# Gate matrices from two-byte one-hots in three parts, with eight more early strips, in a two-layer model kernel

## The chip, the cores and the metric

One core of one Trainium2 chip runs the whole program as one launch. The metric is device time in microseconds, median of several runs on the chip; the kernel before takes 3077.76 us (median of 3, 3073.26 to 3085.12).

## What is computed

The reference is a two-layer model on 512 tokens of width 1024, in float32. Layer one: a mixer (a wide depthwise convolution, a short gated convolution and a spatial gate between two matrix products), a product-key expert layer (PEER), and an embedding gate; then a state-space mixer, a gated feed-forward, another embedding gate, differential attention, a second feed-forward and gate, and a final norm. The change lies almost wholly in the expert layer:

```
q = (nf @ w_q).reshape(t, 8, 256)
s1, s2 = q[..., :128] . sub_keys[:, 0],  q[..., 128:] . sub_keys[:, 1]   # 128 scores each
v1, i1 = top_k(s1, 16);  v2, i2 = top_k(s2, 16)
vals, ci = top_k((v1[..., :, None] + v2[..., None, :]).reshape(t, 8, 256), 16)
idx = i1[ci // 16] * 128 + i2[ci % 16]          # 128 experts of 16384 for each token
gates = softmax(vals)
act = gelu(x . expert_u[idx]) * gates
out = sum_k act * expert_v[idx]
```

## The kernel before, in words

Activations lie features on partitions, tokens along the free dimension. Matrix products are made to nearly float32 accuracy from three fp32r products (`mm3`, L159: high and low part of the weights, high and low part of the input). A *strip* is 1024 rows by 128 columns of weights, 512 KB, loaded on SP's queue (`dma_to`, L128), split into parts on ScalarE (L148) and on VectorE or GpSimd (L150), and used in 24 products.

Program order is written by hand. After each strip `tick` (L97) runs what `later(n, f)` (L92) has put n ticks ahead, and `run_bg` (L200) then issues background items from a list, each with a cost, until the credit given for a strip is used. Every engine runs its instructions in this order.

The expert layer treats block 0 of 128 tokens by gathering rows (`first_block`, L965) and the other 384 tokens densely, over all 16384 experts in 128 strips of `expert_u` and 128 of `expert_v`:

- Stage one (`peer`, L624): the queries, the scores, the top 16 of each half, and the first 9 dense `expert_u` strips. The bias table of the attention is prepared here too (`bias_prep`, L1741), in the background.
- The gates stage: `plan_choice` (L781) picks the experts. `top` takes the best 16 of 50 candidate pairs of a head; `look` (L835) turns a candidate number into an expert number by a one-hot comparison (L838, VectorE), a product with the codes (L841, GpSimd) and a sum over the candidates (L845, VectorE). `soft`, `soft2` make the gates, `ints` (L854) splits an expert number into e1 and e2 of 128 each, and `trans` (L865) turns e1, e2 and the gates on TensorE so that the 128 choices of a token lie on partitions, with the token along the free dimension. `plan_gates` (L878) then makes, for eight tokens at a time, 48 times, the dense gate matrix G[e2, e1] of each token: `front` writes the one-hot of e2 (L894), a one-hot of e1 (L902) and its product with the gate (four tokens on ScalarE, L906, four on VectorE, L908), `mid` makes one fp32 product a token (L917), and `back` copies it on ScalarE (L924) into `gb`, from which pieces go to DRAM (L932). Numbers 0 to 127 for the comparisons are held in a bank of PSUM of their own (`iotaP`, L641).
- Meanwhile TensorE has R - 9 = 47 further `expert_u` strips, whose gelu (L705) is stored to DRAM (`sd`). R = 56 (L575) strips are thus made early; `ahead` (L601) spreads them over the 128. The background credit of a strip is the sum of the costs divided by the strips (L732). 32 row steps of block 0 (`early`, L982: a gather and a dot product) are mixed into blocks 2 and 3 of the background.
- The dense stage (`dense`, L1033): for each e, the `expert_u` strip where it was not made early (gelu L1086, then the gate product L1076), or a load of its stored gelu; then 18 products with the strip of `expert_v` into six banks (L1112). The rest of block 0 and the preparation of the state-space layer run in the background.

Elsewhere: `lin2` (L183) makes the first two strips of a stage from inputs that are only just being written, the first all but its last part, then the second; with `first`, used once, it interleaves the two. `head_ln` and `two_rms` (L332, L355) are the normalisation by head of the mixer, a chain of TensorE, ScalarE and VectorE steps one tick apart; L444 starts it when a convolution is done.

Of the kernel before, what the change touches and what calls it, by code (L numbers as in the profile page):

```python
# [36 lines left out]
class K:  # L37
# [294 lines left out]
    def head_ln(self, y, out):  # L332
# [22 lines left out]
    def two_rms(self, sq, sel, scale, out):  # L355
# [28 lines left out]
        self.later(1, turn)  # L384
# [14 lines left out]
    def mix_in(self, after):  # L399
# [32 lines left out]
        def conv(j, sg):  # L432
# [4 lines left out]
            def tap(k):  # L437
# [5 lines left out]
                if k == 0:  # L443
                    self.later(1, lambda: self.head_ln(acc, lambda yn: ln_a(j, yn)))  # L444
# [82 lines left out]
        self.lin2(xn, posts[o[0]], posts[o[1]], first=True)  # L527
# [47 lines left out]
    R = 56  # L575
    EARLY = 32
    SLOW = 1.6
    RB = 1
    GG = 4
    TC = 32  # L580
    HT = 8
    NV = 4
# [41 lines left out]
    def peer(self):  # L624
# [16 lines left out]
        iotaP = self.bank("mmc", (P, P), "held")  # L641
# [7 lines left out]
        self.bg = self.bias_prep() + [(0.1, lambda: nc.scalar.copy(iotaP, iota))]  # L649
# [131 lines left out]
    def plan_choice(self, vals, idx, iota, rc):  # L781
# [5 lines left out]
        self.eT = e1T, e2T, gT = [loc((P, TD), tag=t) for t in ("e1T", "e2T", "gT")]  # L787
        state = {}

        def part(b, half):  # L790
# [42 lines left out]
            sh = [P, 16, NCD]  # L833

            def look(h):  # L835
                if h < 4 * half + 4:
                    eq = loc((P, 16, NCD), tag="eq", bufs=1 + self.LG)
                    nc.vector.tensor_tensor(  # L838
                        eq, d["i"][:, h, :].unsqueeze(2).to_broadcast(sh), iota[:, 0:NCD].unsqueeze(1).to_broadcast(sh), ALU.is_equal
                    )  # L840
                    nc.gpsimd.tensor_tensor(eq, eq, d["k"][:, h, :].unsqueeze(1).to_broadcast(sh), ALU.mult)  # L841
                    d["eq", h] = eq
# [7 lines left out]
            if not half:  # L850
                return items
            items.insert(len(items) - 3, (0.5, soft2))

# [11 lines left out]
            def trans():  # L865
                pt = self.px_((P, 3, P), "pt")
# [4 lines left out]
                for j, t in enumerate((e1T, e2T, gT)):  # L871
# [6 lines left out]
    def plan_gates(self, part, iota, iotaP, gd, step):  # L878
# [3 lines left out]
        A = HT - self.NV  # L882
        e1T, e2T, gT = self.eT
# [5 lines left out]

        def front(i):  # L890
            t0 = i * HT
            sh = [P, HT, P]
            oh2 = self.loc((P, HT, P), tag="oh2", bufs=2)
            nc.vector.tensor_tensor(  # L894
                oh2, e2T[:, t0 : t0 + HT].unsqueeze(2).to_broadcast(sh), iotaP.unsqueeze(1).to_broadcast(sh), ALU.is_equal
            )
            gh = self.loc((P, HT, P), tag="gh", bufs=2)
            A = HT - self.NV
            if A:
                oh1 = self.loc((P, P, A), BF16, tag="oh1", bufs=2)  # L900
                sh1 = [P, P, A]
                nc.vector.tensor_tensor(oh1, e1T[:, t0 : t0 + A].unsqueeze(1).to_broadcast(sh1), iotaP.unsqueeze(2).to_broadcast(sh1), ALU.is_equal)  # L902
            for t in range(HT):
                e1, g = e1T[:, t0 + t : t0 + t + 1], gT[:, t0 + t : t0 + t + 1]
                if t < A:
                    nc.scalar.activation(gh[:, t, :], oh1[:, :, t], AF.Copy, scale=g)  # L906
                else:
                    nc.vector.tensor_scalar(out=gh[:, t, :], in0=iota, scalar1=e1, scalar2=g, op0=ALU.is_equal, op1=ALU.mult)  # L908
# [29 lines left out]
        bg = part(1, 1)  # L938
        nxt = {1: choose(0) + choose(2), 2: choose(3), 3: []} if self.EARLY else {1: choose(2), 2: choose(3), 3: choose(0)}
        rows = [(1.2, lambda i=i: step(i)) for i in range(self.EARLY)]  # L940
        for b in range(1, NB):
# [7 lines left out]
            for j in range(k):  # L949
# [6 lines left out]
                m = -(-len(more) // (k - j))  # L956
                bg += more[:m]
                more = more[m:]
        bg += [(0.0, lambda: mid(n - 1)), (0.0, lambda: back(n - 2)), (0.0, lambda: back(n - 1)), (0.0, rest)]
# [73 lines left out]
    def dense(self, nr, gd, sd, xd, step):  # L1033
# [707 lines left out]
    def bias_prep(self):  # L1741
# [8 lines left out]
        def loads():  # L1750
            nc.gpsimd.memset(rb, 1e30)
# [429 lines left out]
```

## Time and profile before

| | |
|---|---|
| Median of 3 runs | 3077.76 us (3073.26 to 3085.12) |
| Profiled execution, its own time | 3078.27 us |
| Span of its trace, first to last instruction | 3076.5 us |
| Granted TensorE clock, mean | 0.971 of full |
| TensorE busy | 2908.9 us, 95% |
| VectorE, ScalarE, GpSimd busy | 2218.9, 1303.4, 1093.8 us |
| DRAM read, written | 468.75, 63.44 MB |

Busy time is the union of an engine's instructions, so it hides differences between stages; matrix products are pipelined, and their rate is read from start to start. A wait is put down to what came last before the instruction started. An idle engine costs nothing unless the engine that bounds the stage waits for it.

### The profile page before, as it was taken

The numbers are of one execution on the slowest core, as the hardware profiler recorded it, in microseconds if no ns is written. First come the engines' busy times: TensorE is split into PE (matmuls) and PEld (weight loads), VectorE is DVE, ScalarE is ACT, GpSimd is POOL, SyncE is SP. The second block draws the span as 40 slices with busy tenths as digits, with TensorE's granted clock in tenths as the row PEclk, the third lists the DMA queues.
The fourth block names the chain that finished last, engine by engine and source line by source line (L and its number), as shares of the span: only waits on it lengthen the run. The fifth ranks groups of instructions, "written<-read, shape, count | busy, mean of one in ns | idle before, by whom it ended". The sixth has DMA issues, their size and how long they took to land. (4 is left out here: it accounts for less than half of the span.)

```text
span 3076.5 us, 39413 instructions
## 1 busy us (share of the span) xinstructions
PE 2908.9 (95%) x14359; PEld 2445.6 (79%) x14359; DVE 2218.9 (72%) x3788; ACT 1303.4 (42%) x2209; POOL 1093.8 (36%) x936
## 2 busy tenths in 40 slices
PE   8999988889999999999999979999999998999998
PEld 6677888788887888888787768888877766888886
DVE  7945888986888889988886674666666356566665
ACT  4333246566433433443335343433344345433333
POOL 3224566653248778877872321000011011100001
PEclk9889999899999999999999989999999989999999
DMA  4124335679778988898894473233332211333323
GB/s 140 48 83 148 97 129 186 232 245 313 252 263 313 336 318 322 331 350 315 312 328 147 125 225 103 77 102 99 99 97 95 77 42 42 96 103 96 96 72 99
DMA packets 235067, 534.77 MB, mean 174 GB/s; under 512 B 35135, under 2 KB 127683, under 8 KB 222202
## 3 DMA queue, kind: packets, MB, share of 16 engines
q1 hardware_dynamic: 170570, 343.69, 33.9%
q0 software_dynamic: 24832, 140.74, 12.4%
q10 hardware_dynamic: 39472, 47.84, 4.5%
q8 instruction: 113, 1.85, 0.2%
q14 instruction: 80, 0.66, 0.1%
HBM read 468.75 MB, written 63.44 MB: 173 GB/s over the span
## 5 line engine op out<-in xcount | busy, mean ns | idle before, releaser
L150 DVE TENSOR_TENSOR wl<-wr,wh 128x1024 fp32r<-128x1024 f32 (+2 forms) x453 | 545.3, 1213 | 510.1 <-ACT wh L148 509.9
L148 ACT ACTIVATE wh<-wr 128x1024 fp32r<-128x1024 f32 (+2 forms) x552 | 544.7, 995 | 403.7 <-PE mm L163 196.2
L161 PE MATMUL mm<-xn,wh 128*128 128x512 f32 x1296 | 520.9, 402 | 14.3 <-ACT xn L119 8.9
L163 PE MATMUL mm<-xn,wh 128*128 128x512 f32 x1296 | 512.4, 395 | 5.8 <-DVE xn L114 5.8
L162 PE MATMUL mm<-xn,wl 128*128 128x512 f32 x1296 | 512.1, 395 | 1.9 <-POOL wl L150 1.9
L230 POOL TENSOR_TENSOR accs<-accs,sq 128x512 f32<-128x512 f32 x56 | 86.3, 1541 | 1042.7 <-ACT sq L229 1038.4
L1112 PE MATMUL pv<-wh,A 128*128 128x512 f32 x1536 | 437.5, 397 | 15.8 <-ACT A L117 5.9
L150 POOL TENSOR_TENSOR wl<-wr,wh 128x1024 fp32r<-128x1024 f32 x99 | 241.3, 2439 | 449.1 <-ACT wh L148 446.6
L161 PE MATMUL mm<-n,wh 128*128 128x384 f32 x1024 | 350.6, 342 | 0.8 <-ACT gs L705 0.8
L162 PE MATMUL mm<-n,wl 128*128 128x384 f32 x1024 | 345.6, 337 | 5.9 <-DVE wl L150 4.3
L1112 PEld LDWEIGHTS pv<-wh,A 128*128 128x128 f32 x1536 | 286.8, 189 | 80.6 <-DVE A L112 11.0
L163 PE MATMUL mm<-n,wh 128*128 128x384 f32 x1024 | 345.9, 338 | 3.1 <-DVE n L114 3.1
L161 PEld LDWEIGHTS mm<-xn,wh 128*128 128x128 f32 x1296 | 248.5, 192 | 69.3 <-ACT xn L119 8.9
L163 PEld LDWEIGHTS mm<-xn,wh 128*128 128x128 f32 x1296 | 247.7, 191 | 61.4 <-DVE xn L114 8.3
L162 PEld LDWEIGHTS mm<-xn,wl 128*128 128x128 f32 x1296 | 248.4, 192 | 55.2 <-POOL wl L150 2.3
L1112 PE MATMUL pv<-wl,A 128*128 128x512 f32 x768 | 241.9, 396 | 9.4 <-DVE wl L150 9.3
L117 ACT ACTIVATE A<-ga 128x384 fp32r<-128x384 f32 x128 | 67.3, 526 | 357.7 <-DVE ga L1076 357.7
L162 PEld LDWEIGHTS mm<-n,wl 128*128 128x128 f32 x1024 | 194.2, 190 | 9.7 <-DVE wl L150 5.6
L161 PEld LDWEIGHTS mm<-n,wh 128*128 128x128 f32 x1024 | 194.5, 190 | 4.9 <-issue 1.4
L163 PEld LDWEIGHTS mm<-n,wh 128*128 128x128 f32 x1024 | 194.0, 189 | 3.4 <-DVE n L114 3.4
L1112 PEld LDWEIGHTS pv<-wl,A 128*128 128x128 f32 x768 | 144.0, 189 | 49.0 <-DVE wl L150 17.3
L1670 ACT ACTIVATE uc<-up,vec 128x512 f32<-128x512 f32 x88 | 71.8, 816 | 203.8 <-DVE up L1668 203.8
(414 smaller groups left out, 5438.9 us busy)
## 6 DMA issues: line engine op xcount, KB each, us to landing
wr<-in_exp_u SPq DMA_DIRECT2D x128, 512.0 KB, 5.4
wr<-in_exp_v SPq DMA_DIRECT2D x128, 512.0 KB, 6.9
wr<-in_w_up SPq DMA_DIRECT2D x88, 512.0 KB, 3.6
gd<-gb ACTq DMA_DIRECT2D x48, 512.0 KB, 5.0
G<-gd SPq DMA_DIRECT2D x32, 768.0 KB, 6.3
wr<-in_w_dn SPq DMA_DIRECT2D x64, 320.0 KB, 2.9
wr<-in_w_pg SPq DMA_DIRECT2D x24, 512.0 KB, 4.2
sd<-gs SPq DMA_DIRECT2D x56, 192.0 KB, 2.9
```

What stands on the lines that cost most here:

```text
L117: nc.scalar.activation(hi, src, AF.Copy)
L148: nc.scalar.activation(s.hi, s.raw, AF.Copy)
L150: eng.tensor_tensor(s.lo, s.raw, s.hi.bitcast(F32), ALU.subtract)
L161: t.matmul(ps, wh, xh, start=start, stop=False)
L162: t.matmul(ps, wl, xh, start=False, stop=False)
L163: t.matmul(ps, wh, xl, start=False, stop=stop)
L230: self.later(1, lambda: nc.gpsimd.tensor_tensor(acc, acc, sq, ALU.add))
L1112: nc.tensor.matmul(pv[2 * b + h], a[:, x, o], w[:, h * T : h * T + T], start=(e == 0 and i == 0 and w is s.hi), stop=last)
L1670: nc.scalar.activation(c, u, AF.Identity, scale=w(2), bias=cb[:, m : m + 1])
```

## The change

- Gates: the one-hots of e2 and e1 are written as bfloat16 for all eight tokens in one instruction each, in the order (pair of tokens, number, token of the pair), so that two neighbouring elements lie side by side. The gate is split into three bfloat16 parts that sum to it (`part1` to `part3`), and the one-hot of e1 is multiplied by each: three VectorE instructions. The numbers and the turned gates (`gP`) are bfloat16 in the held bank of PSUM. `mid` makes three products a token, accumulated, and writes a token into every fourth word of the bank, so that `back` copies runs of four words in order.
- `look` compares in bfloat16 with the candidates outermost, GpSimd writes float32, and the sum reads with a step of 16 words.
- R is 64; the last 8 of the 32 row steps come after the last gates (`TAIL`). `trans` of a block stands at the end of the block before, with three items between it and `ints` in the first case; the other items end one step earlier.
- The gelu of a dense strip stays in PSUM (`p_s`), and the gate product reads it there.
- `lin2` always interleaves. In the mixer, `head_ln` starts two ticks after its convolution, and its turn comes two ticks after the statistics.
- The loads of the bias table are issued at once at the start of the expert layer, and its sign is changed on VectorE.

```
-    def lin2(self, rhs, *posts, first=False):
+    def lin2(self, rhs, *posts):
...
-        if first:
-            for k in range(n + 1):
-                for i, j in ((0, k), (1, k - 2)):
-                    if 0 <= j < n - 1:
-                        self.prod(pss[i], ss[i], rhs, j, j + 1)
-        else:
-            for s, ps in zip(ss, pss):
-                self.prod(ps, s, rhs, 0, n - 1)
+        for k in range(n + 1):
+            for i, j in ((0, k), (1, k - 2)):
+                if 0 <= j < n - 1:
+                    self.prod(pss[i], ss[i], rhs, j, j + 1)
...
-            self.later(1, lambda: self.two_rms(d["sq"], self.sel2, 1.0, scale))
+            self.later(1, lambda: self.two_rms(d["sq"], self.sel2, 1.0, scale, 2))
...
-    def two_rms(self, sq, sel, scale, out):
+    def two_rms(self, sq, sel, scale, out, lag=1):
...
-        self.later(1, turn)
+        self.later(lag, turn)
...
-                    self.later(1, lambda: self.head_ln(acc, lambda yn: ln_a(j, yn)))
+                    self.later(2, lambda: self.head_ln(acc, lambda yn: ln_a(j, yn)))
...
-    R = 56
+    R = 64
+    TAIL = 8
...
-        iotaP = self.bank("mmc", (P, P), "held")
+        held = self.bank("mmc", (P, T), "held").bitcast(BF16)
+        iotaP = held[:, 0 : 2 * P].rearrange("p (e b) -> p e b", b=2)
+        self.gP = held[:, 2 * P : 8 * P].rearrange("p (c k t) -> p c k t", c=2, k=3)
+        self.identB = self.loc((P, P), BF16, tag="identB")
+        nc.scalar.copy(self.identB, self.ident)
...
-        self.bg = self.bias_prep() + [(0.1, lambda: nc.scalar.copy(iotaP, iota))]
+        bias, loads = self.bias_prep()
+        loads()
...
+        self.bg = [(0.1, hold)] + bias
...
                 if h < 4 * half + 4:
-                    eq = loc((P, 16, NCD), tag="eq", bufs=1 + self.LG)
+                    eq = loc((P, NCD, 16), BF16, tag="eq", bufs=2)
                     nc.vector.tensor_tensor(
-                        eq, d["i"][:, h, :].unsqueeze(2).to_broadcast(sh), iota[:, 0:NCD].unsqueeze(1).to_broadcast(sh), ALU.is_equal
+                        eq.rearrange("p c (a b) -> p c a b", b=2),
+                        d["i"][:, h, :].rearrange("p (a b) -> p a b", b=2).unsqueeze(1).to_broadcast(sh),
+                        iota[:, 0:NCD, :].unsqueeze(2).to_broadcast(sh),
+                        ALU.is_equal,
                     )
-                    nc.gpsimd.tensor_tensor(eq, eq, d["k"][:, h, :].unsqueeze(1).to_broadcast(sh), ALU.mult)
+                    ec = loc((P, NCD, 16), tag="ec", bufs=1 + self.LG)
+                    nc.gpsimd.tensor_tensor(ec, eq, d["k"][:, h, :].unsqueeze(2).to_broadcast([P, NCD, 16]), ALU.mult)
...
-                    nc.vector.tensor_reduce(d["e"][:, h, :], d["eq", h], AX.X, ALU.add)
+                    nc.vector.tensor_reduce(d["e"][:, h, :], d["eq", h].rearrange("p c k -> p k c"), AX.X, ALU.add)
...
+                nc.scalar.copy(d["gp"][:, 0, :], d["gf"])
...
+                nc.gpsimd.tensor_tensor(d["gr"], d["gf"], d["gp"][:, 0, :], ALU.subtract)
+                nc.scalar.copy(d["gp"][:, 1, :], d["gr"])
...
+                nc.gpsimd.tensor_tensor(d["gp"][:, 2, :], d["gr"], d["gp"][:, 1, :], ALU.subtract)
...
-                nc.tensor.transpose(pt[:, 2, :], d["g"].rearrange("p a b -> p (a b)"), self.ident)
+                for j in range(3):
+                    nc.tensor.transpose(self.gP[:, b % 2, j, :], d["gp"][:, j, :], self.identB)
...
+        H2 = HT // 2
+        pairs = lambda t: t.rearrange("p (a b) -> p a b", b=2).unsqueeze(2).to_broadcast([P, H2, P, 2])
...
+            num = iotaP.unsqueeze(1).to_broadcast([P, H2, P, 2])
+            oh2 = self.loc((P, H2, P, 2), BF16, tag="oh2", bufs=2)
+            nc.vector.tensor_tensor(oh2, pairs(e2T[:, t0 : t0 + HT]), num, ALU.is_equal)
+            oh1 = self.loc((P, H2, P, 2), BF16, tag="oh1")
+            nc.vector.tensor_tensor(oh1, pairs(e1T[:, t0 : t0 + HT]), num, ALU.is_equal)
+            gh = self.loc((P, 3, H2, P, 2), BF16, tag="gh", bufs=2)
+            for k in range(3):
+                nc.vector.tensor_tensor(gh[:, k], oh1, pairs(self.gP[:, b % 2, k, o : o + HT]), ALU.mult)
...
-                pg = self.px_((P, 4, P), "pg")
+                pg = self.px_((P, P, 4), "pg")
                 for t in range(4 * q, 4 * q + 4):
-                    nc.tensor.matmul(pg[:, t % 4, :], oh2[:, t, :], gh[:, t, :], start=True, stop=True)
+                    for k in range(3):
+                        nc.tensor.matmul(pg[:, :, t % 4], oh2[:, t // 2, :, t % 2], gh[:, k, t // 2, :, t % 2], start=(k == 0), stop=(k == 2))
...
-                copy(gb[:, c % 2, :, o : o + 4].rearrange("p e t -> p t e"), pg)
+                copy(gb[:, c % 2, :, o : o + 4], pg)
...
+        rows, last = rows[: self.EARLY - self.TAIL], rows[self.EARLY - self.TAIL :]
...
+            if b in turn:
+                bg.append(turn[b])
...
-                s = self.tmp((P, TD), tag="gs")
-                nc.scalar.activation(s, ps, AF.Gelu_apprx_tanh)
-                gated(e, s)
+                nc.scalar.activation(ps, ps, AF.Gelu_apprx_tanh)
+                gated(e, ps)
```

## Rows read from the trace of the kernel before

**Rows 1.** The page's part 1: busy us, share of the span, instructions.
```profile
PE 2908.9 (95%) x14359; PEld 2445.6 (79%) x14359; DVE 2218.9 (72%) x3788; ACT 1303.4 (42%) x2209; POOL 1093.8 (36%) x936
```
**Rows 2.** Busy time by stretch: the gates stage, the dense stage.
```profile
core 0: us, PE busy (x) PEld busy (x) DVE busy (x) ACT busy (x) POOL busy (x), PEclk, DMA share, GB/s
413.00:755.00 342.00, 294.24 (x1845) 287.38 (x1846) 297.34 (x675) 221.77 (x396) 191.52 (x142) 0.94 0.63 216
755.00:1652.00 897.00, 867.46 (x4206) 747.86 (x4205) 757.94 (x960) 351.96 (x633) 601.80 (x574) 0.99 0.86 309
```
**Rows 3.** Waits of TensorE, 413 to 755 us: total, times, longest.
```profile
PE pg L917 <- ACT gb L924: 30.9, 20, 6.3
PE pt L867 <- DVE ef L863: 10.2, 2, 6.4
PE pt L867 <- ACT gb L924: 5.7, 1, 5.7
```
**Rows 4.** Groups by line and shape, 413 to 755 us: busy, mean ns | idle before.
```profile
L924 ACT COPY gb<-pg 128x512 f32<-128x512 f32 x96 | 94.8, 1092 | 0.1
L908 DVE TENSOR_SCALAR gh<-iota,e1T,gT 128x128 f32<-128x128 f32 x192 | 83.7, 498 | 0.0
L906 ACT ACTIVATE gh<-oh,gT 128x128 f32<-128x128 bf16 x192 | 62.9, 398 | 111.7 <-DVE oh L902 107.0 <-PE mm L162 2.2 <-issue 1.8
L894 DVE TENSOR_TENSOR oh<-e2T,held 128x1024 f32<-128x1024 f32 x48 | 58.1, 1211 | 14.0 <-PE pg L917 9.4 <-ACT e2T L872 4.6
L902 DVE TENSOR_TENSOR oh<-e1T,held 128x512 bf16<-128x512 f32 x48 | 32.5, 678 | 0.0
L845 DVE TENSOR_REDUCE ee<-eq 128x16 f32<-128x800 f32 x24 | 23.1, 977 | 11.2 <-POOL eq L841 11.1
L838 DVE TENSOR_TENSOR eq<-ci,held 128x800 f32<-128x800 uint16 x24 | 22.7, 978 | 0.0
```
**Rows 5.** TensorE in order of time: strip products, 18 from first to last; a gate group.
```profile
500.13 0.33 PE L161 MATMUL mm<-n,wh 128*128 128x384 f32 x1
...
503.07 0.34 PE L163 MATMUL mm<-n,wh 128*128 128x384 f32 x1
...
513.75 1.93 PEld L917 LDWEIGHTS pg<-gh,oh 128*128 128x128 f32 x16
515.60 0.19 PEld L161 LDWEIGHTS mm<-n,wh 128*128 128x128 f32 x1
```
**Rows 6.** Line L1009 by itself, VectorE: ns min/median/max, first and last start.
```profile
L1009 DVE TENSOR_SCALAR gx<-x,first x1: 746/746/746, 782.8 to 782.8; 128x1024 f32<-128x1024 f32 x1
```
**Rows 7.** Lines L1508 (step of 8 words in both sources) and L417, VectorE.
```profile
L1508 DVE TENSOR_TENSOR u<-mm,rstd x8: 1072/1112/1187, 1742.0 to 1793.9; 128x512 f32<-128x512 f32 x8
...
L417 DVE TENSOR_TENSOR val<-mm,rstd x5: 677/684/691, 29.6 to 139.5; 128x512 f32<-128x512 f32 x5
```
**Rows 8.** ScalarE: a plain copy (line L666); strips in the window (413 to 755).
```profile
L666 ACT COPY q<-mm x16: 562/572/593, 245.5 to 377.5; 128x512 f32<-128x512 f32 x16
...
L705 ACT ACTIVATE gs<-mm 128x384 f32<-128x384 f32 x45 | 21.1, 472 | 0.0
```
**Rows 9.** The dense stage, 755 to 1652 us: splits on VectorE, and TensorE's longest wait.
```profile
L150 DVE TENSOR_TENSOR wl<-wr,wh 128x1024 fp32r<-128x1024 f32 x201 | 267.9, 1350 | 126.7 <-ACT wh L148 126.7
...
PE pv L1112 <- DVE wl L150: 9.3, 14, 1.5
```
**Rows 10.** Waits of TensorE, 0 to 415 us: total, times, longest.
```profile
PE pmn L339 <- DVE cacc L442: 6.2, 1, 6.2
PE pst L374 <- DVE rl L369: 3.8, 1, 3.8
PE pb L1761 <- DMA rboh<-in_c_buckets: 3.3, 1, 3.3
```
**Rows 11.** TensorE in order of time at two later seams, idle before in brackets.
```profile
1728.71 0.79 PE L163 MATMUL mm<-xn,wh 128*128 128x512 f32 x1 [2.41 <-DVE xn L114]
...
2350.52 0.50 PE L163 MATMUL mm<-xn,wh 128*128 128x512 f32 x1 [2.03 <-DVE xn L114]
```

More of the change, by code (lines that the diff above doesn't have):

```diff
@@ L526, in mix_in @@
         o = self.W_IN_ORDER
-        self.lin2(xn, posts[o[0]], posts[o[1]], first=True)
+        self.lin2(xn, posts[o[0]], posts[o[1]])
         for m in o[2:]:
@@ L581 @@
     HT = 8
-    NV = 4
     CV = 4
@@ L648, in peer, with hold, turn, again @@
         nc.scalar.dma_start(sk, I["skT"])
-        self.bg = self.bias_prep() + [(0.1, lambda: nc.scalar.copy(iotaP, iota))]
+        bias, loads = self.bias_prep()
+        loads()
+        turned = self.loc((P, 2, P), BF16, tag="turned")
+        def hold():
+            twice = self.tmp((P, P, 2), tag="twice")
+            nc.scalar.copy(twice, iota.unsqueeze(2).to_broadcast([P, P, 2]))
+            flat = twice.rearrange("p a b -> p (a b)")
+            def turn():
+                pt = self.px_((P, 2, P), "pt")
+                for j in range(2):
+                    nc.tensor.transpose(pt[:, j, :], flat[:, j * P : j * P + P], self.ident)
+                self.later(1, lambda: again(pt))
+            def again(pt):
+                nc.scalar.copy(turned, pt)
+                self.later(1, lambda: [nc.tensor.transpose(held[:, j * P : j * P + P], turned[:, j, :], self.identB) for j in range(2)])
+            self.later(1, turn)
+        self.bg = [(0.1, hold)] + bias
         zero = self.loc((P, 112), tag="zero")
@@ L786, in plan_choice @@
         loc = lambda shape, dt=F32, tag="l", bufs=1: pk.tile(list(shape), dt, tag=tag, name=self.name(tag), bufs=bufs)
-        self.eT = e1T, e2T, gT = [loc((P, TD), tag=t) for t in ("e1T", "e2T", "gT")]
+        self.eT = e1T, e2T = [loc((P, TD), BF16, tag=t) for t in ("e1T", "e2T")]
         state = {}
@@ L851, in part, with part1, part2, part3 @@
                 return items
+            def part1():
+                d["gp"] = loc((P, 3, P), BF16, tag="gp")
+                d["gf"] = d["g"].rearrange("p a b -> p (a b)")
+                nc.scalar.copy(d["gp"][:, 0, :], d["gf"])
+            def part2():
+                d["gr"] = self.tmp((P, P), tag="gr")
+                nc.gpsimd.tensor_tensor(d["gr"], d["gf"], d["gp"][:, 0, :], ALU.subtract)
+                nc.scalar.copy(d["gp"][:, 1, :], d["gr"])
+            def part3():
+                nc.gpsimd.tensor_tensor(d["gp"][:, 2, :], d["gr"], d["gp"][:, 1, :], ALU.subtract)
             items.insert(len(items) - 3, (0.5, soft2))
+            if b:
+                for i, f in enumerate((part1, part2, part3)):
+                    items.insert(len(items) - 2 + i - (i == 2), (0.1, f))
             def ints():
@@ L888, in plan_gates @@
         n = TD // HT
+        H2 = HT // 2
+        pairs = lambda t: t.rearrange("p (a b) -> p a b", b=2).unsqueeze(2).to_broadcast([P, H2, P, 2])
         def front(i):
             t0 = i * HT
[L892 to L908, printed above, removed]
+            b, o = 1 + t0 // P, t0 % P
+            num = iotaP.unsqueeze(1).to_broadcast([P, H2, P, 2])
[6 more added lines that the diff above has]
+                nc.vector.tensor_tensor(gh[:, k], oh1, pairs(self.gP[:, b % 2, k, o : o + HT]), ALU.mult)
             F[i] = oh2, gh
@@ L936, in rest @@
                 put()
-        bg = part(1, 1)
         nxt = {1: choose(0) + choose(2), 2: choose(3), 3: []} if self.EARLY else {1: choose(2), 2: choose(3), 3: choose(0)}
+        turn = {0: part(1, 1), 1: nxt[1], 2: nxt[2]}
+        turn = {b: (x, x.pop())[1] for b, x in turn.items()}
+        bg = part(1, 1)[:-1] + nxt[1][:3] + [turn[0]]
+        nxt[1] = nxt[1][3:]
         rows = [(1.2, lambda i=i: step(i)) for i in range(self.EARLY)]
+        rows, last = rows[: self.EARLY - self.TAIL], rows[self.EARLY - self.TAIL :]
         for b in range(1, NB):
@@ L955, in plan_gates @@
                     bg.append((0.0, lambda i=i: back(i - 2)))
-                m = -(-len(more) // (k - j))
+                m = -(-len(more) // max(1, k - 1 - j))
                 bg += more[:m]
                 more = more[m:]
-        bg += [(0.0, lambda: mid(n - 1)), (0.0, lambda: back(n - 2)), (0.0, lambda: back(n - 1)), (0.0, rest)]
+            if b in turn:
+                bg.append(turn[b])
+        bg += [(0.0, lambda: mid(n - 1)), (0.0, lambda: back(n - 2)), (0.0, lambda: back(n - 1)), (0.0, rest)] + last
         self.bg += bg
@@ L1772, in lam @@
             nc.vector.tensor_scalar(out=self.nlam, in0=self.nlam, scalar1=-self.LAM_INIT, scalar2=None, op0=ALU.add)
-        return [(0.1, loads)] + [(0.1, lambda h=h: head(h)) for h in range(8)] + [(0.1, lam)]
+        return [(0.1, negate)] + [(0.1, lambda h=h: head(h)) for h in range(8)] + [(0.1, lam)], loads
     def head_rms(self, y, gain, then):
```

18 lines of the change are left out of this document (9 added, 9 removed).

## The prediction

> **What bounds the kernel now.** I began with busy time by engine: TensorE is busy for 2908.9 us of a span of 3076.5 [rows 1], so what can go is TensorE work, TensorE's idle time (168 us), or time at a low clock. Busy time by stretch then separates two stages that this change rearranges [rows 2]. In the gates stage (413 to 755 us) TensorE works 294.2 of 342 us at a granted clock of 0.94, and VectorE 297.3: neither is full, they wait for each other. In the dense stage (755 to 1652) TensorE works 867.5 of 897 us and sets the pace. The waits of TensorE in the gates stage say how [rows 3]: 30.9 us for ScalarE's copy of a gate bank (L924), 5.7 more for the same copy ahead of a transpose, 10.2 for VectorE's integer expert numbers. ScalarE is late because it stands in order behind its own gate products (L906), which sat idle 107.0 us for VectorE's one-hot L902 [rows 4]. So the loop is VectorE, ScalarE, PSUM bank, TensorE. The reader should see that ScalarE's busy time (221.8 us of 342 [rows 2]) is no bound, but its place in the loop is.
>
> **Gates on TensorE.** The old pass: 16 passes of a group of eight tokens start at 513.75 and the next work at 515.60 [rows 5], 1.85 us, 0.116 us a pass; 48 groups are 89 us at full clock. New: eight tokens by three parts, 24 products a group, 1152 in all. No row has a two-byte product, so I bound it. Below: the strip products run one pass of 384 columns each in (503.07 - 500.13)/17 = 0.173 us [rows 5], 0.00045 us a column, so 128 columns take 0.058 us and all 1152 take 66 us. Above: the old pass, 0.116, which also loads 128 weights for 128 columns; 133 us. I take 0.07, 81 us, nearer the strip because a two-byte product should need one pass, and above it because each product still loads weights for only 128 columns and now writes every fourth word of its bank. [...]
>
> **Gates on VectorE.** Removed per group: L894 1.211 us, L902 0.678, four L908 at 0.498 mean; 48 groups are 58.1 + 32.5 + 83.7 = 174.3 us [rows 4]. Added: five TENSOR_TENSOR of 1024 two-byte elements, one operand in PSUM, 240 in all. At today's rate each costs L894's 1.211 us (same count, same bank). The rows L894 and L902 give (1.211 - 0.678)/512 = 0.00104 us an element and 0.145 fixed; with two elements in the time of one an instruction costs 0.145 + 0.533 = 0.68 us. Bounds: 163 us and 291 us. That VectorE can go so fast at all is shown by a one-source instruction only: 1024 elements in 0.746 us [rows 6]. I take 0.68, since all operands and the result are two-byte and come in adjacent pairs; that leaves VectorE 11 us lighter. [...]
>
> **The look-up.** The comparison L838 becomes two-byte: 0.978 to 0.145 + 0.417 = 0.56 us, 24 in the stage, -10 us at best, 0 at worst. The sum L845 now reads with a step of 16 words. A strided read costs 1.112 us against 0.684 for 512 elements [rows 7], 0.0008 us an element; for 800 that is +0.67 us (two strided sources there, one here, so +0.33 as the other end), 24 times +8 to +16 us. Together I count 0 for VectorE; GpSimd's product stays at 800 elements and is covered.
>
> **ScalarE.** L906 goes (62.9 us), and L924 writes runs of four words instead of scattering: a plain copy of the same size takes 0.572 us [rows 8] against 1.092, 96 times, -50 us; if short runs cost as much as scattered words, 0. The two-byte transposes, the parts of the gates, the held numbers and the identity are a few instructions a block, under 4 us in the stage on any engine; TensorE's writes of the gates into the held bank must wait for VectorE's reads of it, three times, with the next strip and gate group queued behind them on TensorE; I price each at half of the old number waits of 10.2 us at worst, and at 2 us as taken, since the number transposes in front of them wait for VectorE anyway.
>
> **Eight strips move.** R goes from 56 to 64. A strip is 24 x 0.173 = 4.14 us of TensorE, so the dense stage loses 33 us and the gates stage, 45 strips in the window [rows 8], gains 33. In the dense stage its DMA share of 0.86 [rows 2] and the splits on VectorE (1.350 us each [rows 9]) fill a shorter stage; there TensorE already waits 9.3 us for them, so I take 3 back: -30 us. Each strip also issues one more weight load, one store and one load of 192 KB on SP's queue; the gates stage's DMA share is 0.63, and they hide there. The gelu in place costs VectorE nothing: one PSUM operand of 512 takes 0.684 us [rows 7]. It holds its bank until VectorE's product is done, under 1 us later, and the next strip but one, some 8 us on, is the first to want it.
>
> **Sum for the gates stage.** TensorE: 53 x 4.14 = 219 + 81 + about 4 for transposes = 304. VectorE: 297 - 11 + 0 = 286, so TensorE is the longer for the first time. The 36.6 us of copy waits lose their cause; what is late next is VectorE in the first block, where two other blocks' choices fall. For that and the held bank I leave 16 us of waits, and for time at a low clock 8: today's 294.2 busy against 45 x 4.14 + 89 = 275 is 19 us of it. 304 + 16 + 8 = 328, against 342: -14 us.
>
> **The seams.** In the mixer one wait of 6.2 us and one of 3.8 [rows 10] get a strip (about 5 us) put in front of them; VectorE is behind there, so I count 7 of 10 and +1 at the end of the mixer, where two more steps fall into the drain: -6. The bucket load, 3.3 [rows 10], is issued earlier: -3. With it three small loads and a memset move to the front of GpSimd's queue, ahead of its zero stores, which nothing in the stage reads; the negation that follows goes to VectorE, one instruction of eight columns. The number wait at 413 (part of 10.2) gets three items ahead of it: -3. The interleaved pair of strips spreads waits such as 2.41 and 2.03 us [rows 11]: -4. The last eight row steps move behind the last gates, so the stores finish earlier, -2. Together -18 us, between 0 and -26.
>
> Total: -14 - 30 - 18 = -62 us on the profiled execution's 3078.3 (span and 1.8 around it), which lies 0.5 above the median of 3077.8: **3016 us**.
>
> **Rivals.** *TensorE pays the old pass price.* If the strided write or the weight load sets the pace, 1152 x 0.116 = 133 us. For: the old gate row has the same 128 by 128 shape. Against: it makes two passes per product. Stage: 219 + 133 + 4 + 16 + 8 = 380, +38; total 38 - 30 - 18 = -10: 3068, no change to be told. [...]
>
> *VectorE stays at one element at a time.* The price of a pair instruction decides. At 1.211 us the 240 take 291 us, VectorE's stage is 297 - 174 + 291 + 11 for the strided sums = 425, and with 10 us of waits 435, +93; total 93 - 30 - 18 = +45: 3123. It turns slower where the stage passes 390 us, at 240p = 390 - 10 - 134, p = 1.02 us. For: nothing in this trace shows an instruction of two tensors at the faster rate. Against: the one-source row.
>
> *Everything at the low end.* 66 us on TensorE, waits and low clock of 8 us together: 219 + 66 + 4 + 8 = 297, -45; with -33 for the dense stage and -24 at the seams, 2976.
>
> *The strips bring nothing*: if the dense stage gave back half, 3031; inside the range.
>
> **How the numbers follow.** Forecast 0.58, old pass price 0.20, one element at a time 0.12, all at the low end 0.10. A measurement here can tell about 0.5%, 15 us: faster is below 3062, slower above 3093. Faster: 0.58 + 0.10 + 0.08 of the old-price case, whose own spread of 20 us reaches below 3062, is 0.76; same 0.12; slower 0.12. The range runs from the low case to the middle of the old-price case, 2982 to 3076, and leaves out the slower case and the tails.
>
> **What would show it.** Right: L924 near 0.6 us, the pair instructions near 0.68, 24 products of a group in about 1.7 us, TensorE's waits for `gb` gone, the gates stage 320 to 335 us with eight strips more, the dense stage near 867. Wrong: pair instructions at 1.2 us and VectorE full through the gates stage; or a group taking 2.8 us with TensorE full; or the dense stage unshortened with its idle time grown by what the strips took out.

## The result, and the profile after

The kernel after takes 3057.41 us (median of 6, 3051.30 to 3064.58) against 3079.68 (median of 6, 3070.24 to 3090.27): ratio 0.9925, 95% interval 0.9904 to 0.9947. That is faster by 0.75%, some 22 us, where 62 were forecast. The profiled execution has a span of 3056.1 us, 20.4 us under the span before.

First busy time and the two stages, as in [rows 1] and [rows 2]: the page's part 1, then the stretches (us; busy time of each engine with its instructions; granted clock, DMA share, GB/s).

```profile
PE 2931.8 (96%) x14753; PEld 2468.3 (81%) x14753; DVE 2194.8 (72%) x3733; ACT 1209.8 (40%) x2022; POOL 1100.3 (36%) x949
```
```profile
404.00:757.00 353.00, 348.76 (x2425) 341.19 (x2424) 290.06 (x613) 136.82 (x220) 208.73 (x150) 1.00 0.69 233
757.00:1636.00 879.00, 837.47 (x3987) 715.12 (x3985) 738.26 (x950) 340.04 (x615) 591.29 (x572) 0.98 0.86 309
```

In the gates stage TensorE is now busy 348.8 of 353 us at full granted clock: the loop of VectorE, ScalarE and PSUM banks is gone, and TensorE alone sets the time. In the dense stage, taken from the first to the last product with `expert_v` (landmarks below), TensorE has 26 us less to do and the stage is only 12 us shorter.

The costs of the new instructions, by line and shape, 404 to 757 us (count, busy us, mean ns, idle before), for [rows 4]:

```profile
L958 PE MATMUL pg<-gh,oh 128*128 128x128 bf16 x1152 | 133.6, 309 | 0.7 <-DVE gh L947 0.7
...
L947 DVE TENSOR_TENSOR gh<-oh,held 128x1024 bf16<-128x1024 bf16 x144 | 90.3, 682 | 1.7
L965 ACT COPY gb<-pg 128x512 f32<-128x512 f32 x96 | 54.9, 585 | 50.1 <-PE pg L958 45.2 <-DMA gd<-gb 4.9
L868 POOL TENSOR_TENSOR ec<-eq,code 128x800 f32<-128x800 bf16 x24 | 39.0, 1637 | 31.5 <-DVE eq L861 31.4
L872 DVE TENSOR_REDUCE ee<-ec 128x16 f32<-128x800 f32 x24 | 36.9, 1554 | 0.0
L942 DVE TENSOR_TENSOR oh<-e2T,held 128x1024 bf16<-128x1024 bf16 x48 | 32.7, 680 | 37.4 <-PE pg L958 32.4 <-ACT e2T L917 4.7 <-issue 0.2
L944 DVE TENSOR_TENSOR oh<-e1T,held 128x1024 bf16<-128x1024 bf16 x48 | 32.5, 678 | 0.0
L861 DVE TENSOR_TENSOR eq<-ci,held 128x800 bf16<-128x800 uint16 x24 | 13.0, 561 | 0.0
```

VectorE's pair instructions take 0.680 us, the comparison 0.561, ScalarE's copy 0.585: each as costed. The waits have turned round: VectorE now waits 32.4 us for TensorE to free its one-hots (L942), and ScalarE 45.2 us for gate sums (L965). The price of TensorE's products is read from start to start, TensorE in order of time (start, duration):

```profile
504.83 2.79 PE L958 MATMUL pg<-gh,oh 128*128 128x128 bf16 x24
507.38 0.42 PE L161 MATMUL mm<-n,wh 128*128 128x384 f32 x1
```

2.55 us for 24 products (2.52 by their weight loads), 0.106 us each, one pass to a product (x1152 in the groups above); so 48 groups take 122 us in place of the 81 forecast. The old pass, read the same way from product to product in the trace of the kernel before:

```profile
513.93 1.95 PE L917 MATMUL pg<-gh,oh 128*128 128x128 f32 x16
515.63 0.42 PE L161 MATMUL mm<-n,wh 128*128 128x384 f32 x1
```

1.70 us for 16 passes, 0.106 us each as well; the prediction's 0.116 was read between weight loads [rows 5]. But the old passes, of four-byte operands, write their sums side by side.

Waits of TensorE in the dense stage after (total us, times, longest), for [rows 9]:

```profile
PE pv L1160 <- DVE wl L150: 20.0, 19, 5.9
PE pv L1160 <- ACT wh L148: 10.5, 5, 3.9
PE pv L1160 <- DVE A L112: 7.1, 6, 2.1
PE pv L1160 <- ACT A L117: 3.8, 1, 3.8
```

VectorE's splits are waited for 20.0 us, where it was 9.3. By landmarks of TensorE in both traces:

| us | before | after | gained | forecast |
|---|---|---|---|---|
| start to first transpose of numbers | 413.8 | 401.8 | 12.0 | 12 |
| from there to the first product with `expert_v` | 349.5 | 355.5 | -6.0 | 14 |
| first to last product with `expert_v` (dense) | 890.3 | 878.4 | 11.9 | 30 |
| from there to the end | 1422.9 | 1420.4 | 2.5 | 6 |

So two terms failed, the gates stage by 20 us and the dense stage by 18. The 12 us ahead of the gates came in full, in other places than forecast (last experiments).

### The profile page after: what moved, and what is told of

The parts are those of the page before. It is cut to its first block, busy times and chain, and to the rows that moved or that the text cites. A ratio compares the mean times of both kernels' runs of the same rounds, so it can differ in the third digit from the quotient of the medians.

```text
span 3056.1 us, 39894 instructions
## 1 busy us (share of the span) xinstructions
PE 2931.8 (96%) x14753; PEld 2468.3 (81%) x14753; DVE 2194.8 (72%) x3733; ACT 1209.8 (40%) x2022; POOL 1100.3 (36%) x949
## 5 line engine op out<-in xcount | busy, mean ns | idle before, releaser
L150 DVE TENSOR_TENSOR wl<-wr,wh 128x1024 fp32r<-128x1024 f32 (+2 forms) x445 | 538.5, 1220 | 494.6 <-ACT wh L148 493.9
L161 PE MATMUL mm<-xn,wh 128*128 128x512 f32 x1296 | 517.6, 399 | 13.4 <-ACT xn L119 8.1
L150 POOL TENSOR_TENSOR wl<-wr,wh 128x1024 fp32r<-128x1024 f32 x107 | 259.3, 2426 | 422.2 <-ACT wh L148 416.9
L161 PE MATMUL mm<-n,wh 128*128 128x384 f32 x1024 | 348.9, 341 | 0.0
L161 PEld LDWEIGHTS mm<-xn,wh 128*128 128x128 f32 x1296 | 247.1, 191 | 67.1 <-ACT xn L119 8.1
L161 PEld LDWEIGHTS mm<-n,wh 128*128 128x128 f32 x1024 | 194.4, 190 | 3.5 <-issue 1.2
```

Source lines behind the costliest of these rows:

```text
L150: eng.tensor_tensor(s.lo, s.raw, s.hi.bitcast(F32), ALU.subtract)
L161: t.matmul(ps, wh, xh, start=start, stop=False)
```

## The price of a gate product

All of these are edits of the kernel after, at its line 958 and, where the bank's layout changes, at the bank and ScalarE's copy of it.

**Half the moving columns, half the weights.**

```
-for k in range(3):
-    nc.tensor.matmul(pg[:, :, t % 4], oh2[:, t // 2, :, t % 2], gh[:, k, t // 2, :, t % 2], start=(k == 0), stop=(k == 2))
+for h in range(2):
+    e = slice(64 * h, 64 * h + 64)
+    for k in range(3):
+        nc.tensor.matmul(pg[:, e, t % 4], oh2[:, t // 2, :, t % 2], gh[:, k, t // 2, e, t % 2], start=(k == 0), stop=(k == 2))
```

> Each gate product is made as two, with the same 128 weight columns and 64 moving columns each; the output is complete. After the change a group of 24 products took 2.52 us from start to start, 0.105 us a product. If the load of 128 weight columns (or a fixed price a product) sets that, 48 products take about 5.0 us a group, the gates stage grows by about 120 us and the kernel takes about 3180 us. If the stream of the moving columns or the writes of the sums set it, half the columns cost half, the group stays at about 2.5 us and the time at about 3057 us.

```
+        nc.tensor.matmul(pg[e, :, t % 4], oh2[:, t // 2, e, t % 2], gh[:, k, t // 2, :, t % 2], start=(k == 0), stop=(k == 2))
```

> Each gate product is made as two, with 64 weight columns each and the same 128 moving columns; the output is complete. If the weight load sets the 0.105 us and goes with the number of columns, the group of now 48 products stays near 2.5 us and the time near 3057 us. If a fixed price a product or the stream of 128 moving columns sets it, the group takes about 5.0 us and the kernel about 3180 us. Load with this run and the one before: this 2.5, that 5.0; stream: this 5.0, that 2.5; fixed price: both 5.0.

TensorE in order of time with half the moving columns, then with half the weights:

```profile
505.55 2.85 PE L960 MATMUL pg<-gh,oh 128*128 128x64 bf16 x48
508.21 0.42 PE L161 MATMUL mm<-n,wh 128*128 128x384 f32 x1
```
```profile
502.49 2.81 PE L960 MATMUL pg<-gh,oh 128*64 128x128 bf16 x48
505.23 0.44 PE L161 MATMUL mm<-n,wh 128*128 128x384 f32 x1
```

2.66 and 2.74 us for twice as many products; 3065.82 and 3074.38 us in one run each. No theory gave both: a load of 128 weights would cost 5.0 in the first, the stream of 128 columns 5.0 in the second, a fixed price 5.0 in both. The first run rules out the load and the fixed price. In the second something happened that its expectation had not reckoned with. The mean durations of the products (ns, behind the busy time), first with half the columns, then with half the weights; and two short windows of the second run, 0.014 and 0.115 us long, with the products in them:

```profile
L960 PE MATMUL pg<-gh,oh 128*128 128x64 bf16 x2304 | 136.4, 247 | 0.7 <-DVE gh L947 0.7
L960 PE MATMUL pg<-gh,oh 128*64 128x128 bf16 x2304 | 134.2, 310 | 0.3 <-DVE gh L947 0.3
```
```profile
502.49 0.30 PE L960 MATMUL pg<-gh,oh 128*64 128x128 bf16 x2
502.49 0.41 PE L960 MATMUL pg<-gh,oh 128*64 128x128 bf16 x4
```

A product with half the weights lasts as long as a whole one (310 ns; 309 in the kernel after), but two run at a time: in this trace the two that write different halves of the partitions start 1 to 6 ns apart, and the next two 0.109 us after them, which is the step from one product to the next in the kernel after. So half the weights alone save nothing, and both runs leave the moving columns: their stream, or the writing of their sums.

**Where the sums lie.** In the kernel after a product writes every fourth word of its bank.

```
-pg = self.px_((P, P, 4), "pg")
+pg = self.px_((P, 4, P), "pg")
...
-nc.tensor.matmul(pg[:, :, t % 4], oh2[:, t // 2, :, t % 2], gh[:, k, t // 2, :, t % 2], start=(k == 0), stop=(k == 2))
+nc.tensor.matmul(pg[:, t % 4, :], oh2[:, t // 2, :, t % 2], gh[:, k, t // 2, :, t % 2], start=(k == 0), stop=(k == 2))
...
-copy(gb[:, c % 2, :, o : o + 4], pg)
+copy(gb[:, c % 2, :, o : o + 4].rearrange("p e t -> p t e"), pg)
```

The next run does this and reads the operands side by side as well (in each, 128 elements from t x 128 on):

> The 24 products of a group read 128 weights and 128 moving columns that lie side by side and write sums that lie side by side; the columns so read are of several tokens, so the gates are not those of the reference, but the number and size of all operations are the same. ScalarE then copies from the other layout. If the steps between elements (4 bytes in the pairs, 16 in the sums) slow the load or the stream, the group falls from 2.52 us towards 24 x 0.06 to 0.07 = 1.4 to 1.7 us and the kernel gets 20 to 40 us faster. If they don't matter, the group stays at 2.4 to 2.6 us and the time at 3050 to 3065 us.

This one does only what the diff shows:

> Only the sums in PSUM lie side by side for each token; weights and moving columns stay in pairs, and the output is complete. If the 16-byte step of the sums sets the price of a product, the group falls below 2 us here as in the run with all steps of one; if the steps of the operands do, only that run falls and this one stays at 2.5 us; if none does, both stay.

They took 3026.51 and 3028.43 us, in one run each. Timed, the second edit gives:

> The kernel after with the sums of the gates side by side in PSUM, as in the one look before, now timed. If the one look was typical, 3025 to 3032 us, a ratio to the kernel before of 0.982 to 0.986; the time saved against the kernel after (3057 us) is then 25 to 32 us of the 56 us that TensorE is relieved of.

3025.81 us (4 runs), ratio to the kernel before 0.9822, interval 0.9786 to 0.9858. TensorE in order of time, first with all steps one word, then with the sums alone side by side (the profiled one of the four runs):

```profile
485.25 1.51 PE L958 MATMUL pg<-gh,oh 128*128 128x128 bf16 x24
486.57 0.42 PE L161 MATMUL mm<-n,wh 128*128 128x384 f32 x1
```
```profile
484.58 1.55 PE L958 MATMUL pg<-gh,oh 128*128 128x128 bf16 x24
485.94 0.42 PE L161 MATMUL mm<-n,wh 128*128 128x384 f32 x1
```

1.32 and 1.36 us a group: the steps of the sums are the whole of it, those of the operands a hundredth or so. A product costs 0.056 us. TensorE is relieved of 48 x 1.19 = 57 us, the kernel of about 32; the rest is covered by what comes next. The same run's gates stage by stretch, ScalarE's copy among its groups, and TensorE's waits in it:

```profile
404.00:728.50 324.50, 300.56 (x2427) 288.91 (x2426) 290.36 (x616) 180.08 (x220) 207.50 (x151) 0.98 0.74 255
```
```profile
L965 ACT COPY gb<-pg 128x512 f32<-128x512 f32 x96 | 99.6, 1153 | 14.4 <-PE pg L958 13.9 <-DMA sd<-gs 0.5
```
```profile
PE pg L958 <- DVE gh L947: 6.9, 18, 0.7
PE held L914 <- DVE gh L947: 5.2, 2, 2.6
PE mm L162 <- POOL wl L150: 4.8, 4, 1.6
PE mm L162 <- DVE wl L150: 4.6, 1, 4.6
```

324.5 us: TensorE 300.6, VectorE 290.4, and TensorE now waits 24 us, mostly for VectorE. ScalarE's copy scatters again and takes 1.153 us; ScalarE is busy 180 of 324 us with it, and of TensorE's waits for gate banks only 1.5 us are put down to ScalarE. The old layout of the bank was thus the better one: the change moved the scattered side from ScalarE, which had room, to TensorE, which had none.

**The smallest step that costs.**

```
-pg = self.px_((P, P, 4), "pg")
+pg = self.px_((P, 2, P, 2), "pg")
...
-nc.tensor.matmul(pg[:, :, t % 4], oh2[:, t // 2, :, t % 2], gh[:, k, t // 2, :, t % 2], start=(k == 0), stop=(k == 2))
+nc.tensor.matmul(pg[:, t % 4 // 2, :, t % 2], oh2[:, t // 2, :, t % 2], gh[:, k, t // 2, :, t % 2], start=(k == 0), stop=(k == 2))
...
-copy(gb[:, c % 2, :, o : o + 4], pg)
+copy(gb[:, c % 2, :, o : o + 4].rearrange("p e (a b) -> p a e b", b=2), pg)
```

> The sums of a gate product lie 8 bytes apart in PSUM (two tokens in turn), in place of 16 after the change and 4 in the runs with sums side by side. A group of 24 products took 2.52 us at 16 bytes and about 1.35 us at 4. If any step but that of one word halves the rate, the group takes 2.5 us and the kernel 3050 to 3062 us. If 8 bytes still go at full rate, 1.35 us and 3022 to 3032 us. If the price goes with the bytes spanned, about 1.7 us and about 3035 us.

```profile
505.42 2.79 PE L958 MATMUL pg<-gh,oh 128*128 128x128 bf16 x24
507.97 0.42 PE L161 MATMUL mm<-n,wh 128*128 128x384 f32 x1
```

2.55 us and, in one run, 3054.89 us: 8 bytes cost as much as 16. Of the three steps tried, 4, 8 and 16 bytes, only that of 4 gave 0.056 us a product; at 8 and 16 it was 0.106.

## Eight strips less in the dense stage

**Each part alone.** `R = 56` in the kernel after; `R = 64` in the kernel before; and the gelu back in SBUF:

```
-    nc.scalar.activation(ps, ps, AF.Gelu_apprx_tanh)
-    gated(e, ps)
+    s = self.tmp((P, TD), tag="gs")
+    nc.scalar.activation(s, ps, AF.Gelu_apprx_tanh)
+    gated(e, s)
```

> The kernel after with 56 early strips as before, so 8 strips (24 x 8 x 0.173 us = 33 us of TensorE) go back from the gates stage to the dense stage. Theory A (the dense stage is held by VectorE's splits and the gathers, so fewer strips there bring little; all else in the change leaves it alone): dense stage 888 to 893 us as before, gates stage 355 - 33 = 322 to 332 us, kernel 3034 to 3045 us. Theory B (the dense stage does get 33 us shorter by 8 strips, and the gelu in PSUM or another part of the change lengthens it by 21 us): dense stage 911 us, kernel 3055 to 3065 us.

> The kernel before with 64 early strips and nothing else of the change. The gates stage of before has 48 of 342 us in which TensorE is idle. Theory A (8 strips less shorten the dense stage by 10 to 15 us alone): dense stage 875 to 881 us, gates stage longer by between 0 (all in the idle time) and 33 us, kernel 3066 to 3100 us. Theory B (33 us less, taken back by other parts of the change): dense stage 857 us, kernel 3046 to 3080 us.

> The kernel after with the gelu of a dense strip put into SBUF as before. Theory A (few strips moved bring little, the place of the gelu is not it): dense stage 875 to 881 us, kernel 3052 to 3062 us. Theory B (the gelu in PSUM took back 21 us): dense stage about 857 us, kernel about 3036 us.

| | us, median (runs) | ratio to before, 95% | dense stage, us | TensorE idle in it, us |
|---|---|---|---|---|
| before (56) | 3076.11 (14) | | 890.3 | 27.7 |
| before with 64 | 3080.55 (10) | 1.0016 [1.0001, 1.0031] | 881.8 | 43.3 |
| after (64) | 3057.41 (6) | 0.9925 [0.9904, 0.9947] | 878.4 | 41.5 |
| after with 56 | 3048.63 (4) | 0.9898 [0.9866, 0.9930] | 893.9 | 30.9 |
| after, gelu in SBUF | 3056.13 (5) | 0.9920 [0.9893, 0.9947] | 882.2 | 44.2 |

(Idle is the stage less TensorE's busy time in it.) The eight strips shorten the dense stage by 8.5 us in the old kernel and by 15.5 in the new one, and each time TensorE's idle time grows by 11 to 16; the place of the gelu changes nothing that can be told. A single trace of this stage says it to some 6 us: in the ten traces in which its code is that of the kernel after (it, and the nine runs here that change only other stages) it takes 872.4 to 883.9 us, 878.3 in the mean, while the three with 56 strips take 890.3 to 894.8. So the two gains can't be told apart, and the move is worth some 15 us of the 33. The kernel before gains nothing from it: its gates stage grows from 349.5 to 360.1 us. The kernel after is faster without it, median against median by 9 us (the intervals overlap), which with TensorE full in the gates stage was to be expected: 3048.63 is 4 us above the range of theory A, since the gates stage fell to 336.6 us and not to 322 to 332. The dense stages of the two kernels with 56 strips, stretch by stretch:

```profile
763.30:1653.60 890.30, 862.64 (x4175) 743.07 (x4176) 756.12 (x958) 349.83 (x630) 598.36 (x571) 0.99 0.85 309
```
```profile
739.70:1633.60 893.90, 863.02 (x4176) 748.31 (x4176) 742.29 (x958) 352.21 (x630) 591.29 (x571) 0.99 0.86 308
```

and after, with 64:

```profile
757.30:1635.70 878.40, 836.87 (x3986) 714.82 (x3984) 737.97 (x949) 339.90 (x614) 590.99 (x572) 0.98 0.86 309
```

The strips' 33 us appear as 26 us of TensorE's busy time (the granted clock is 0.98 in place of 0.99), of which 14 turn into idle time.

**What takes them back.** Two cuts of the kernel after, alone and together: in `fetch` only the u half of a row (its index, twice the number of the expert, is written once by VectorE), in `step` every second sum over v left out.

```
+    elif j % 2 and E < j < 3 * E + 1:
+        gather(slot(j)[:, 0 : 8 * P], half, self.two[:, 0, (j - E) // 2 : (j - E) // 2 + 1])
...
-    if j > 1:
+    if j > 1 and (j % 2 == 0 or j < 4):
         add(j - 2)
```

> The kernel after, but 32 of the 96 gathers of whole rows in the dense stage fetch only the u half of each row (0.5 MB in place of 1 MB); the sums over v of those experts use old data, all instructions of the engines stay. Dense stage of the kernel after: 878 us, 271 MB at 309 GB/s. If the traffic with DRAM paces the stage, 16.8 MB less at 309 GB/s are worth up to 54 us; TensorE's own 837 us stop it at about 840 us, so dense 840 to 850 us and kernel 3018 to 3030 us. If VectorE's order of work paces it, dense 870 to 880 us and kernel 3048 to 3060 us (at most the 12 us of VectorE's waits for gathers go).

> The kernel after, but every second product and sum of VectorE over the gathered v rows (line 1060, 1.35 us each) is left out, 62 of 127, so the expert layer of the first 128 tokens lacks half of its experts; all transfers stay. That is 84 of VectorE's 738 us in the dense stage. If VectorE's work paces the stage, dense 840 to 850 us (TensorE's own 837 us stop it) and kernel 3018 to 3030 us. If the traffic with DRAM paces it, dense 870 to 880 us and kernel 3048 to 3060 us.

> The kernel after with both of the earlier cuts of the dense stage: 32 gathers fetch half a row, and 62 of VectorE's sums over gathered rows are left out, so the expert layer of the first 128 tokens is incomplete. Alone they took the dense stage from 878 to 868 and to 864 us. If traffic and VectorE each hold TensorE at other places, the gains add: about 854 us, kernel about 3032 us. If each is the cover of the other, more than that goes: 840 to 848 us, kernel 3018 to 3026 us. If both act on the same waits, or neither is the cause, dense stays at 862 to 866 us.

The dense stages with half rows, with half the sums, and with both:

```profile
758.50:1626.80 868.30, 831.89 (x3984) 712.80 (x3983) 740.25 (x950) 338.75 (x614) 613.84 (x572) 0.99 0.83 293
```
```profile
756.10:1620.50 864.40, 833.80 (x3986) 717.22 (x3984) 641.60 (x887) 342.40 (x614) 548.31 (x572) 0.98 0.87 314
```
```profile
757.50:1607.00 849.50, 824.62 (x3984) 709.89 (x3984) 648.20 (x887) 341.86 (x614) 560.29 (x572) 0.99 0.84 300
```

868.3, 864.4 and 849.5 us, the kernel 3049.09, 3041.71 and 3030.67, in one run each. Both single forecasts fell: neither the traffic nor VectorE's work paces the stage by itself. Against 878.4 us they give 10 and 14 us, and together 29. The single cuts end only 4 and 8 us below the shortest of the ten traces with the whole work, so each of these two gains is weakly shown, and whether together they do more than add is not shown; both together end 23 us below it, which is clear. The waits for the splits on VectorE fall from 20.0 us to 17.8 with half the rows and to 7.1 with half the sums. With both cuts TensorE idles 24.9 us, less than before the change, and its busy time is 12 us shorter too, at a granted clock of 0.99 in place of 0.98.

## The part ahead of the gates

> The kernel after with the loads of the bias table issued from the background again, just ahead of the sign change, as before. The gain ahead of the first scores was 9.4 us (254.0 to 244.6 us), though the wait for this load was 3.3 us; in the kernel before the 14.6 us behind that wait ran at a granted clock of 0.65. If the wait brought the low clock with it, the wait of about 3 us comes back, the clock behind it falls, and the first scores come 7 to 11 us later, at 252 to 256 us. If only the wait was the load's, they come at 247 to 249 us.

```
-        loads()
...
-        self.bg = [(0.1, hold)] + bias
+        self.bg = [(0.1, hold), (0.1, loads)] + bias
```

> The kernel after with the two shifts of the mixer undone: the normalisation starts one tick after its convolution and its turn one tick after the statistics. The mixer ended at 189.9 us before and at 189.7 after, against a forecast of 6 us less. If the shifts did nothing because VectorE holds the mixer, it ends at 189 to 191 us here too, with the old waits for the sums of the convolution and for the deviations (6.2 and 3.8 us) back. If they gained 6 us that another part of the change took back, it ends at about 196 us.

```
-            self.later(1, lambda: self.two_rms(d["sq"], self.sel2, 1.0, scale, 2))
+            self.later(1, lambda: self.two_rms(d["sq"], self.sel2, 1.0, scale))
...
-                    self.later(2, lambda: self.head_ln(acc, lambda yn: ln_a(j, yn)))
+                    self.later(1, lambda: self.head_ln(acc, lambda yn: ln_a(j, yn)))
```

| start, us | before | after | late loads | mixer undone |
|---|---|---|---|---|
| last product of the mixer's output (`mm<-mix`, L161) | 224.4 | 224.2 | 222.0 | 220.6 |
| first scores (`sc<-sk,q`) | 254.2 | 244.8 | 245.5 | 241.2 |
| between | 29.8 | 20.6 | 23.5 | 20.6 |

In the kernel before, the stretch behind the 3.3 us wait for the bucket load (at 239 us, [rows 10]); in the kernel after the same stretch:

```profile
239.40:254.00 14.60, 14.48 (x43) 10.34 (x44) 1.29 (x2) 5.75 (x11) 7.23 (x6) 0.65 0.47 144
```
```profile
239.00:254.00 15.00, 15.00 (x71) 11.64 (x69) 7.92 (x36) 6.67 (x13) 11.43 (x9) 1.00 0.72 233
```

The wait of 3.3 us was followed by a granted clock of 0.65 over 14.6 us: 14.6 x 0.35 = 5.1 us of full clock, so an estimated 8.4 us with the wait. The rest of the 9.2 us is moved work: before the first scores the kernel before makes eight bias products (`pb`), the kernel after four and two short transposes. With the loads late again only a wait of 1.3 us comes back (the sign change, now on VectorE), the clock of 239 to 254 us is 0.89, and 2.9 us are lost: neither expectation's size, but again over twice the wait, and again the wait and what the clock costs (15 x 0.11 = 1.7). Of the 18 traces of all runs, the three in which TensorE waits between 234 and 254 us (3.3, 3.2 and 1.3 us) have a granted clock of 0.74, 0.74 and 0.91 in that stretch, and the other 15 have 1.00. The mixer's shifts gained nothing. Undone, its old waits return (6.2 and 4.3 us) and it ends no later; it ended 3.6 us earlier, of which some 2 us lie within what the same code varies (224.2 against 222.0 in the two runs that share it). After the change TensorE waits 7.3 us for VectorE in their place (waits of TensorE, 0 to 404 us; the first, for `xn`, stood before too):

```profile
PE mm L161 <- ACT xn L119: 8.1, 1, 8.1
PE pmn L335 <- DVE vv L413: 7.3, 2, 6.2
```

## Versions that beat both

With the sums side by side the gates stage has room again, so the number of strips and of parts was tried on it.

`R = 56`:

> Sums of the gates side by side in PSUM, and 56 early strips in place of 64. With 64 the gates stage took 324 us (TensorE busy 301, VectorE 290) and the dense stage 874 us. With 56 TensorE has about 268 us in the gates stage, so VectorE's 290 us and its waits hold it: 305 to 318 us; dense 888 to 894 us as in the other runs with 56. Kernel 3015 to 3035 us. If the gates stage could still follow TensorE, it would be 291 us and the kernel about 3008 us.

3034.15 us (4 runs), ratio 0.9857, interval 0.9840 to 0.9873: gates stage 318.0 us (TensorE 277.7, VectorE 288.6), dense 894.8. VectorE is the busier of the two in the gates stage now, TensorE waits 38 us there for it, and the eight strips fill such gaps: here 64 looks the better number, by 8 us between the medians (the intervals overlap).

Two parts in place of three, with 64 strips:

```
-gh = self.loc((P, 3, H2, P, 2), BF16, tag="gh", bufs=2)
-for k in range(3):
+gh = self.loc((P, 2, H2, P, 2), BF16, tag="gh", bufs=2)
+for k in range(2):
...
-        for k in range(3):
+        for k in range(2):
```

> Sums side by side in PSUM, and the gate products take two of the three bfloat16 parts, so the gates are exact to about 16 bits only. VectorE loses 48 instructions of 0.68 us, 33 us, TensorE 384 products of 0.056 us, 21 us. If VectorE and TensorE hold the gates stage between them (290 and 301 of 324 us), it falls by 18 to 28 us, to 296 to 306 us, and the kernel to 2998 to 3008 us; if something else does (the look-ups on GpSimd, the row gathers), it stays above 312 us and the kernel above 3014 us.

3007.82 us (4 runs), ratio 0.9774, interval 0.9758 to 0.9790: gates stage 304.5 us, within the range. It leaves out the third part of every gate. The version with three parts and the sums side by side computes what the kernel after computes, at 0.9822.

## Why the prediction was wrong

- **Gates on TensorE: the step that failed, by its size.** "I take 0.07, 81 us, nearer the strip": it was 0.106 and 122 us. The prediction named the weight load and the strided write as reasons to go above 0.058 and gave them 0.012 us, a quarter of the gap of 0.048; the strided write is the whole gap (0.056 without it, weight load included). The rival of the old pass price named the strided write too, and its price was within a tenth, but that was luck: it was taken from passes that write side by side. Its 380 us for the stage was too much, since it kept 24 us of waits and low clock, and the full TensorE of the kernel after had hardly any (4.2 us idle, clock 1.00).
- **VectorE and ScalarE: right.** 0.680 us against 0.68, 0.561 against 0.56, 0.585 against "near 0.6". The strided sum took 1.55 in place of 0.977 us, 0.58 more, within the bounds of 0.33 and 0.67. The second rival is dead: a pair instruction took 0.680 us for 1024 two-byte elements, one operand in PSUM, where 1024 four-byte ones took 1.211.
- **The gates stage's sum: off by that term, and by the waits that went with it.** With 0.106 us in place of 0.07 the sum gives 369 us; 353 were measured, TensorE busy 348.8 of them at clock 1.00, so that the 16 us of waits and 8 of low clock shrank to 4.2. With 0.056 it gives 312; 324.5 were measured, with 24 us of waits in place of 16. That TensorE is the longer and VectorE the next was as said.
- **Eight strips move: failed.** "I take 3 back" of 33 us: 17.5 to 24.5 came back with R alone, 21 in the change, as 14 us more idle time of TensorE, much of it behind VectorE's splits, and a granted clock of 0.98 in place of 0.99. I read the waits of the dense stage (9.3 us) as a fixed sum. As I read the runs now, they are what is left of a slack between TensorE and the others, and less work for TensorE uses that slack up; that VectorE's work and the traffic together hold the stage is shown by the run with less of both, the share of each is open. The line that was to show it wrong ("unshortened with its idle time grown") came in part: 12 us shorter, idle time grown by 14.
- **The seams: the sum right, the parts wrong.** Mixer 0 in place of 6; bucket load 9.2 in place of 3, of which the wait and the clock behind it are an estimated 8.4; from the first scores to the numbers 2.6, where 3 were forecast; the end 2.5 in place of 6. A wait in the mixer went, and VectorE was late for the next.
- **The range.** Its ends, 2982 and 3076, are not the two cases that it names, 2976 and 3068.

With the gates stage at +6 and the dense stage at -12 in place of -14 and -30, the forecast of -62 becomes -24; the end's 3.5 us less make it -20.4.

## What to carry to other kernels

When several products share a PSUM bank, try a side-by-side run of words for each and let the reading engine scatter, if that engine has room: here a product took 0.056 us in place of 0.106, and ScalarE's copy 1.153 in place of 0.585. Ask which engine has room before moving a stride from one to the other. Taking work from the engine that paces a stage was worth here, as I read the runs, only the slack that the others had: eight strips, 33 us of TensorE, shortened the dense stage by 8.5 and 15.5 us. So look at how near the others are and test the move alone. And price a wait with the clock of the stretch behind it: here 3.3 us of waiting became an estimated 8.4.

## What the runs showed of the hardware that was not expected

TensorE's products of 128 by 128 two-byte operands took 0.056 us with their weight load when the 128 sums of a partition lay side by side, and 0.106 when they lay 8 or 16 bytes apart. Products of 64 moving columns took 0.055 us each (2.66/48), with sums 16 bytes apart. Products of 64 weights with 128 strided columns that write in turn to the two halves of the partitions ran two at a time: the two of a pair started 1 to 6 ns apart, the next pair after 0.109 us. Steps of 4 bytes between the operands' elements cost 0.001 to 0.002 us a product (1.36 against 1.32 us a group). And a wait of TensorE of 3.3 us cost an estimated 8.4 us, since the granted clock was 0.65 in the 14.6 us behind it; one of 1.3 us, with a clock of 0.89 from 239 to 254 us, cost 2.9.
